# Cosine-similarity attention on one core: the first head pair head by head with its K only cast, the norms of the third and fourth pair by Newton steps, and new instruction orders on every engine

## The chip, the cores and the metric

The kernel runs on one core of a Trainium2 chip. The metric is the time of one execution in device microseconds (us). The kernel before takes 190.31 us, the median of three runs (190.27 to 190.34).

## The reference

Q, K and V are float32 arrays of 8 batches x 12 heads x 512 positions x 64 dimensions, tau is 0.1.

```python
Q_norm = Q / (np.linalg.norm(Q, axis=-1, keepdims=True) + 1e-10)
K_norm = K / (np.linalg.norm(K, axis=-1, keepdims=True) + 1e-10)
scores = np.einsum('bhqd,bhkd->bhqk', Q_norm, K_norm) / tau
weights = np.exp(scores - np.max(scores, axis=-1, keepdims=True))
weights = weights / (np.sum(weights, axis=-1, keepdims=True) + 1e-10)
return np.einsum('bhqk,bhkd->bhqd', weights, V).astype(np.float32)
```

Scores lie between -10 and 10, so the kernel takes exponentials without subtracting the maximum.

## The kernel before

**Work.** The 96 heads are worked in 48 pairs s = 0 to 47 (the text says pair 0 to pair 47, so "third pair" is pair 2). One pair has two heads h and four blocks c of 128 keys; a block's scores are 128 keys x 512 queries for each head. Q (w = 0) and K (w = 1) go through the same steps. For each pair:

- `LD` loads Q and K, 256 KB each (SP queue, L311; pair 0 in halves by head, L308, its K from ScalarE's queue), `LV` loads V (L314). Seventeen pairs of Q and K and ten of V fit in SBUF, so that `LD` of pair s waits for the last readers of pair s-17, and `LV` for the cast of pair s-10.
- `SQ` squares Q and K: one GpSimd instruction for the pair (L337); for pairs 0 to 3 split over ScalarE and GpSimd (L239, L241, L329, L331). `SSQ` adds up the squares of K (of Q too in pairs 1 to 3) in part with matmuls on TensorE (L354), `RED` finishes on VectorE (L361 behind `SSQ`, L365 from the squares, L245 in pair 0).
- `NEW` turns the sums into inverse norms for a group of pairs. Groups 0 to 3 are one pair each, later ones two, and the last one four. Most groups do it with an integer estimate and two Newton steps on VectorE (L389 to L398: `NEW` 0 to 8). The groups in `NORM_ON_ACT` do it on ScalarE: a logarithm `LOG` (L379, in pair 0 L248) and a small exponential of -0.5 times it (`NEW` 7, L382; in pair 0 `NRMS`, L252).
- `SCL` multiplies by the inverse norm and writes bfloat16 (L420; pair 0 L258). Q is done on VectorE, K on GpSimd, except the pairs in `K_ON_DVE`, whose K is done on VectorE too. tau is left to the exponential's scale.
- `TR` transposes on TensorE (L426; pair 0 L266 and L268), `EVA` copies the result to SBUF on VectorE (L434; pair 0 L279).
- `SCO` makes the scores of a block (two matmuls of 512 columns, L508) in one of two pairs of PSUM banks, so a block's score waits for the exponential two blocks earlier. `EXP` takes both heads' exponential in one ScalarE instruction (L531, 128x1024, with immediate scale 1/tau).
- `VC` casts V on GpSimd (L536). `PV` multiplies the exponentials with V and a column of ones, in four parts i of four matmuls for each head (L548). `RCP` and `NRM` divide by the sums on VectorE (L559, L561; last pair L587, L589), `ST` stores 256 KB (L565; last pair L593, in three pieces).

**Pair 0 before.** `head0` (L231) builds it. Both Q and K are scaled by inverse norms (K on GpSimd); the blocks 0 and 1 are done as four half exponentials (one head each, 128x512), the blocks 2 and 3 as full ones.

**The polynomial.** One block, c = 3 of pair 43, takes its exponential without ScalarE: two single matmuls `SCX` (L468), two conversions `X` for each head on VectorE (L473, L475), and six steps `Y` 0 to 5, the first four on GpSimd, the last two on VectorE (L486, L480). `PV` of pair 43 waits for `Y` 5.

**Order.** No scheduler runs at build time. `ORDER` holds one list of numbers per engine (SP, GpSimd, VectorE, TensorE, ScalarE), which is that engine's program in order; a number is the position of an operation in the sequence of `P.add` calls. The texts count the entries of such a list from 0. A negative number in TensorE's list is a filler matmul that only keeps the engine busy. `run()` (L42) derives the semaphore waits from each operation's needs. An engine works strictly in order, so an instruction that waits holds up all behind it in its list. On TensorE and ScalarE, waits for operations of the same engine are dropped unless the operation sets `.own`.

```python
o.waits = [self.ops[n] for n in o.needs]
if e in ("pe", "act") and not o.own:
    o.waits = [p for p in o.waits if p.eng != e]
```

Of the kernel before, what the change touches and what calls it, by code (L numbers as in the profile page):

```python
# [19 lines left out]
class Program:  # L20
# [22 lines left out]
    def run(self):  # L43
# [65 lines left out]
def bass_cosine_similarity_attention_kernel(  # L109
# [44 lines left out]
    t_k0 = sc_ps[:, 3, :].bitcast(bf16)[:, 0:SEQ].rearrange("p (t x) -> p t x", t=NT)  # L154
# [39 lines left out]
    P.fill = lambda e, n: e.matmul(out=sc_ps[:, 0, 0:n], lhsT=ident[:, :], rhs=warm_in[:, 0:n], start=True, stop=True)  # L194
# [26 lines left out]
    before = [[], []]  # L221
# [9 lines left out]
    def head0(TF):  # L231
        for h in range(2):
            at = -100 + h
            x4 = [xs[0][:, 8 * w + 4 * h : 8 * w + 4 * h + 4] for w in range(2)]
            for w in range(2):
# [4 lines left out]
                else:  # L240
# [5 lines left out]
            cols = lambda t, h=h: t[:, 0:16].rearrange("p (w x) -> p w x", w=2)[:, :, 4 * h : 4 * h + 4]  # L246
            P.add(("LOG", 0, h), "act", "ln", at + 0.4, [("RED", 0, 0, h), ("RED", 0, 1, h), "eps", "table"],
                  lambda e, cols=cols: e.activation(out=cols(ys[0]), in_=cols(xs[0]), func=ACT.Ln, bias=eps[:, :]))  # L248
            r_ps = sc_ps[:, 1, 0:4] if h == 0 else n_ps[:, 0, 128:132]
            for w in range(2):  # L250
                P.add(("NRMS", 0, w, h), "act", "sm_act", at + 0.5 + 0.01 * w, [("LOG", 0, h)],
                      lambda e, w=w, h=h, r_ps=r_ps: e.activation(  # L252
                          out=xs[0][:, 8 + 4 * h : 12 + 4 * h] if w else r_ps,
                          in_=ys[0][:, 8 * w + 4 * h : 8 * w + 4 * h + 4], func=ACT.Exp, scale=-0.5)).own = True
            for w in range(2):
                r = x4[1] if w else r_ps
                P.add(("SCL", 0, w, h), "pool" if w else "dve", "sclph" if w else "sclh", at + 0.6 + 0.1 * w, [("NRMS", 0, w, h)],
                      lambda e, w=w, h=h, r=r: e.tensor_tensor(  # L258
                          out=qn[0][:, w, :, h, :], in0=qk[0][:, w, h, :].rearrange("p (t d) -> p t d", t=NT),
                          in1=r.unsqueeze(2).to_broadcast([128, NT, DIM]), op=ALU.mult))  # L260
                out = t_k0 if w else t_ps[:, 0]

                def tr(e, w=w, h=h, out=out):
                    for t in range(NT):
# [7 lines left out]
                      [("SCL", 0, w, i) for i in range(h + 1)] + [("EVA", 0, w, 0) if h else None, "eye"], tr)  # L272
# [20 lines left out]
    def last_direct(s):  # L293
        d = [g for g in NORM_ON_ACT if g > 0 and direct_r(g)]
        return [("NEW", max(d), 7)] if d and group[s] not in NORM_ON_ACT and s < 12 else []

    def pair(s):
# [6 lines left out]
        for w, x in ((0, Q), (1, K)):  # L304
# [5 lines left out]
            P.add(("LD", s, w), "sp", "ld1" if s == 1 else "ld", s, [*([("SCL", 0, w, 0), ("SCL", 0, w, 1), ("SQ", 0, w, 0), ("SQ", 0, w, 1)] if s == R_QK else [key("SCL", s - R_QK, w), *(squares(s - R_QK, w) if s >= R_QK else [])])],  # L310
# [65 lines left out]
        if s == first[g] and g in NORM_ON_ACT:  # L376
# [6 lines left out]
                      out=n_ps[:, g % R_X, 128 : 128 + 2 * m] if direct else xs[g][:, 0 : 2 * m],  # L383
                      in_=ys[g % R_X][:, 0 : 2 * m], func=ACT.Exp, scale=-0.5)).own = True
            if not direct:
                P.add(("NEW", g, 6), "dve", "new", TF - 2.6, [("NEW", g, 7), ("NRMS", 0, 0, 1)],
                      lambda e: e.tensor_copy(out=n_ps[:, g % R_X, 128 : 128 + 2 * m], in_=xs[g][:, 0 : 2 * m]))
        elif s == first[g]:
# [15 lines left out]
            for k, step in enumerate(steps):  # L404
                needs = [("NEW", g, min(k, 6) - 1 if k < 8 else 7)] if k else reds + (free[1] if K_ON_DVE else [])
                if 6 <= k < 8:
                    needs += free[k - 6]
                P.add(("NEW", g, k), "dve", "new", TF - 4.9 - slack(s, M_NEW) + (M_STEP * (k - 7) if s > 8 else 0.23 * k), needs, step)
# [30 lines left out]
    def scos(s):  # L439
# [4 lines left out]
        return [("SCO", s, c) for c in range(NT)] if s else [("SCO", 0, c, h) for c in range(2) for h in range(2)] + [("SCO", 0, 2), ("SCO", 0, 3)]  # L444
# [4 lines left out]
    def exps(s, c):  # L449
# [4 lines left out]
        if s == 0 and c < 2:  # L454
# [39 lines left out]
    def rest(s):  # L494
# [3 lines left out]
        for c in range(NT):  # L498
            if (s, c) in OFF:
                poly(s, c, T0 - 3.0)  # L500
                continue
            turn = chunks.index((s, c))
            b = turn % 2

            for hs in ((0,), (1,)) if s == 0 and c < 2 else ((0, 1),):
                def sco(e, c=c, b=b, hs=hs):
                    for h in hs:
                        last = e.matmul(  # L508
                            out=sc_ps[:, 2 * b + h, :], lhsT=qt[iqt][64 * h : 64 * h + 64, 1, c, :],
                            rhs=qt[iqt][64 * h : 64 * h + 64, 0, :, :], start=True, stop=True)  # L510
                    return last

                needs = [("EVA", s)] if s else [("EVA", 0, w, h) for w in range(2) for h in (hs if c < 2 else (0, 1))]
                needs += exps(*chunks[turn - 2]) if turn >= 2 else []
                needs += [("SCL", 0, 0, 0)] if s == 0 and c == 0 and hs == (1,) else []
                P.add(("SCO", s, c) if len(hs) == 2 else ("SCO", s, c) + hs, "pe", "sco" if len(hs) == 2 else "sco1",
                      T0 + 0.9 * c + (0.5 * hs[0] if len(hs) < 2 else 0), needs, sco)
# [7 lines left out]
            for hs in ((0,), (1,)) if s == 0 and c < 2 else ((0, 1),):  # L525
                one = len(hs) == 1
                P.add(("EXP", s, c) + hs if one else ("EXP", s, c), "act", "exp1" if one else "exp",
                      T0 + 0.9 * c + (0.45 if s else 1.4) * hs[0] * one,
                      [("SCO", s, c) + hs if one and s == 0 else ("SCO", s, c)]
                      + [key("PV", s - R_ET, h, NT - 1) for h in range(2)] + ["table"],  # L530
                      lambda e, c=c, b=b, hs=hs: e.activation(  # L531
                          out=et[iet][:, c, hs[0] : hs[-1] + 1, :], in_=sc_ps[:, 2 * b + hs[0] : 2 * b + hs[-1] + 1, :],
                          func=ACT.Exp, scale=math.log(2.0) / UNIT if s in off_of else inv_tau))
# [9 lines left out]
        for h in range(2):  # L543
            for i in range(NT):
# [9 lines left out]
                need, due = sum((exps(s, c) for c in range(NT)), []), T0 + PERIOD + 0.9 * PV_AT[4 * h + i] + late(s)  # L554
# [64 lines left out]
K_ON_DVE = (1, 2, 3, 4, 9, 15, 21, 27, 33, 39)  # L619
# [20 lines left out]
def slack(s, most):  # L640
# [128 lines left out]
```

## Time and profile before

| what | value |
|---|---|
| median of the runs | 190.31 us |
| span of the profiled execution | 188.2 us |
| ScalarE (ACT) busy | 181.4 us, 96% |
| TensorE (PE) busy | 174.7 us, 93% |
| VectorE (DVE) busy | 169.6 us, 90% |
| GpSimd (POOL) busy | 160.8 us, 85% |
| moved by DMA | 50.75 MB, mean 270 GB/s |
| first half exponential starts | 8.16 us |
| first exponential of pair 1 / pair 2 starts | 12.81 / 16.78 us |
| last exponential ends | 184.86 us |
| last division ends | 186.02 us |

The span is that of one profiled execution, from its first instruction to its last; the 2.1 us between it and the median lie outside of the profile. Busy shares are means over the span. A group's line in the profile gives line, engine, operation, output and input tiles with shapes, the number of instructions, their busy time, the mean duration of one in ns, and the idle time of the engine just before them with what ended most of it. Times of single operations in the texts are read from the trace's timeline; an instruction's duration is longer than the distance to the next one where the two overlap (a full exponential lasts about 1.17 us, and one follows another every 0.917 us).

### The profile page before, as it was taken

Reading aid. Unit: us, or ns where it says so; the run is one execution under the profiler, and the core shown is the slowest. Engines: PE = TensorE matmul, PEld = TensorE weight load, DVE = VectorE, ACT = ScalarE, POOL = GpSimd, SP = SyncE. Lnnn points to the kernel's source line nnn. Section 1 sums busy time; section 2 is a strip of 40 time slices with the busy share of each in tenths; the row PEclk is TensorE's granted clock in tenths of the full one; section 3 lists DMA queues with packets and bytes.
Section 4 is the critical chain, followed back from the end, with each engine's and each line's share of the span. In section 5 each row is a group of like instructions: output and inputs, shape, how many; then the busy total and the mean of one; then the engine's idle time right before and its main releaser. Section 6 shows DMA issues by size and latency. Waiting matters only on the chain.

```text
span 188.2 us, 6658 instructions
## 1 busy us (share of the span) xinstructions
PE 174.7 (93%) x2710; PEld 109.9 (58%) x2710; DVE 169.6 (90%) x537; ACT 181.4 (96%) x213; POOL 160.8 (85%) x149
## 2 busy tenths in 40 slices
PE   6998999999999999999999899999999999797992
PEld 2655665666565666666666566666556566463662
DVE  2789999999999999999999989999899999989653
ACT  4899999999999999999999999999999999999992
POOL 4699989999999999999999999999999993695000
PEclk9999999999999999999999999999999999999999
DMA  5999999999999978999999997989779621111233
GB/s 151 346 353 352 348 358 327 269 331 365 379 382 368 309 236 271 317 360 322 368 380 381 376 317 237 326 292 296 254 215 354 204 73 55 60 56 59 101 125 112
DMA packets 52445, 50.75 MB, mean 270 GB/s; under 512 B 3136, under 2 KB 52416, under 8 KB 52416
## 3 DMA queue, kind: packets, MB, share of 16 engines
q1 hardware_dynamic: 51984, 50.02, 80.7%
q8 instruction: 21, 0.34, 0.7%
q10 hardware_dynamic: 432, 0.33, 0.5%
q14 instruction: 8, 0.07, 0.1%
HBM read 37.75 MB, written 12.58 MB: 267 GB/s over the span
## 4 chain that ended last, share of the span: by engine, by line
ACT 93%; DMA 3%; SPq 1%; issue 1%; PE 1%; DVE 1%
ACT et L531 92%; DMA qk<-in_Q_dram 3%; PE ops L576 1%; SPq L311 0%; SPq L308 0%; ACT ys L379 0%; DVE ob L589 0%; ACT sq L329 0%; ACT nps L382 0%; DVE rd L587 0%; PE tps L576 0%
## 5 line engine op out<-in xcount | busy, mean ns | idle before, releaser
L531 ACT ACTIVATE et<-scps 128x1024 bf16<-128x1024 f32 (+1 forms) x192 | 175.0, 1171 | 0.0
L337 POOL TENSOR_TENSOR sq<-qk 128x1024 bf16<-128x1024 f32 x44 | 82.9, 1900 | 0.7 <-DMA qk<-in_K_dram 0.5
L508 PE MATMUL scps<-qt 64*128 64x512 bf16 x382 | 75.2, 386 | 6.3 <-ACT et L531 3.0
L548 PE MATMUL ops<-vb,et 128*128 128x65 bf16 x1504 | 75.2, 194 | 2.1 <-ACT et L531 1.3
L548 PEld LDWEIGHTS ops<-vb,et 128*128 128x128 bf16 x1504 | 56.5, 98 | 30.8 <-issue 21.0
L420 POOL TENSOR_TENSOR qn<-qk,rk 128x512 bf16<-128x512 f32 x37 | 38.3, 1048 | 6.2 <-DVE rk L394 5.3
L561 DVE TENSOR_TENSOR ob<-ops,rd 128x256 f32<-128x256 f32 x94 | 39.0, 418 | 0.8
L420 DVE TENSOR_TENSOR qn<-qk,nps 128x512 bf16<-128x512 f32 x57 | 38.0, 676 | 0.4 <-ACT nps L382 0.4
L434 DVE COPY qt<-tps 128x1024 bf16<-128x1024 bf16 x47 | 32.2, 685 | 2.2 <-PE tps L426 1.6
L426 PE MATMUL tps<-ident,qn 128*128 128x128 bf16 x376 | 33.4, 220 | 0.1
L508 PEld LDWEIGHTS scps<-qt 64*128 64x128 bf16 x382 | 19.1, 92 | 24.1 <-ACT et L531 9.4
L365 DVE TENSOR_REDUCE nps<-sq 128x8 f32<-128x512 bf16 x46 | 31.0, 681 | 0.0
L536 POOL TENSOR_SCALAR vb<-vf 128x512 bf16<-128x512 f32 x48 | 29.6, 634 | 0.1
L426 PEld LDWEIGHTS tps<-ident,qn 128*128 128x128 bf16 x376 | 21.5, 98 | 10.3 <-issue 3.6
L559 DVE RECIPROCAL rd<-ops 128x4 f32<-128x4 f32 x94 | 16.5, 176 | 6.5 <-PE ops L548 4.2
L354 PE MATMUL ops<-sq,ident 128*128 128x64 bf16 x384 | 19.2, 193 | 0.0
L354 PEld LDWEIGHTS ops<-sq,ident 128*128 128x128 bf16 x384 | 14.4, 98 | 4.3 <-issue 2.7
L361 DVE TENSOR_REDUCE nps<-ops 128x8 f32<-128x64 f32 x42 | 9.0, 214 | 0.5 <-PE ops L354 0.4
L389 DVE TENSOR_TENSOR nps<-nps,ys 128x32 f32<-128x32 f32 (+1 forms) x30 | 6.3, 209 | 0.2
L390 DVE SCALAR_TENSOR_TENSOR nps<-nps,ys 128x32 f32<-128x32 f32 (+1 forms) x30 | 6.2, 208 | 0.2
L191 PE MATMUL ops<-warm_in,ident 128*128 128x512 bf16 x8 | 3.6, 631 | 1.4 <-POOL ident L181 1.4
L331 POOL TENSOR_TENSOR sq<-qk 128x512 bf16<-128x512 f32 (+1 forms) x4 | 3.7, 933 | 0.9 <-DMA qk<-in_K_dram 0.9
(61 smaller groups left out, 54.2 us busy)
## 6 DMA issues: line engine op xcount, KB each, us to landing
vf<-in_V_dram SPq DMA_DIRECT2D x48, 256.0 KB, 5.8
qk<-in_Q_dram SPq DMA_DIRECT2D x47, 256.0 KB, 4.9
qk<-in_K_dram SPq DMA_DIRECT2D x47, 256.0 KB, 6.0
out_dram<-ob SPq DMA_DIRECT2D x47, 256.0 KB, 4.0
qk<-in_Q_dram SPq DMA_DIRECT2D x2, 128.0 KB, 2.7
qk<-in_K_dram ACTq DMA_DIRECT2D x2, 128.0 KB, 3.0
out_dram<-ob SPq DMA_DIRECT2D x1, 128.0 KB, 1.7
out_dram<-ob ACTq DMA_DIRECT2D x1, 64.0 KB, 1.6
```

What stands on the lines that cost most here:

```text
L337: lambda e: e.tensor_tensor(out=sqf, in0=data, in1=data, op=ALU.mult))
L354: last = e.matmul(out=o_ps[bank][:, 320:384], lhsT=ident[:, :], rhs=sq[iqs][:, 8 * w : 8 * w + 8, 8 * k : 8 * k + 8], start=(k == 0), stop ...
L365: lambda e, w=w, dst=dst: e.tensor_reduce(out=dst, in_=sq[iqs][:, 8 * w : 8 * w + 8, :], axis=AX.X, op=ALU.add))
L420: lambda e, w=w, r=r: e.tensor_tensor(out=qn[iqn][:, w].rearrange("p t h d -> p h t d"), in0=qk[iq][:, w].rearrange("p h (t d) -> p h t d" ...
L426: last = e.transpose(t_ps[:, w, t, :], qn[iqn][:, w, t].rearrange("p h d -> p (h d)"), ident[:, :])
L434: lambda e: e.tensor_copy(out=qt[iqt][:, :, :, :].rearrange("p w t x -> p (w t x)"), in_=t_ps[:, :, :, :].rearrange("p w t x -> p (w t x)")))
L508: last = e.matmul(out=sc_ps[:, 2 * b + h, :], lhsT=qt[iqt][64 * h : 64 * h + 64, 1, c, :], rhs=qt[iqt][64 * h : 64 * h + 64, 0, :, :], sta ...
L531: lambda e, c=c, b=b, hs=hs: e.activation(out=et[iet][:, c, hs[0] : hs[-1] + 1, :], in_=sc_ps[:, 2 * b + hs[0] : 2 * b + hs[-1] + 1, :], f ...
L536: lambda e: e.tensor_scalar(out=vb[:, iq, :, :, 0:DIM].rearrange("p c h d -> p h c d"), in0=vf[iv][:, :, :].rearrange("p h (c d) -> p h c ...
L548: last = e.matmul(out=o_ps[h][:, 65 * t : 65 * t + 65], lhsT=et[iet][:, c, h, 128 * t : 128 * t + 128], rhs=vb[:, iq, c, h, :], start=(c = ...
L559: lambda e, h=h, grid=grid: e.reciprocal(out=rd[io][:, h, :], in_=grid[:, :, DIM]))
L561: lambda e, h=h, grid=grid: e.tensor_tensor(out=ob[io][:, h], in0=grid[:, :, 0:DIM], in1=rd[io][:, h, :].unsqueeze(2).to_broadcast([128, N ...
```

## The change

- **Pair 0 head by head.** All four blocks of head 0, then those of head 1, as eight half exponentials (128x512), in four PSUM banks, one for each block. The inverse norm of K is no longer multiplied into K: it is given to the exponential as a scale, a column of SBUF with one value for each partition (each key). So K is only cast to bfloat16 (`CST`, head 0 on ScalarE, head 1 on GpSimd) and transposed, into a bank of the output (`o_ps[0]`) in place of a score bank; pair 0's two `SCL` on GpSimd go. `LOG` is split by Q and K (four instructions of 128x4 for two of 128x8); its scale of 1/inv_tau on the sums gives Q's and K's inverse norms a factor of sqrt(1/tau) each, so that tau lies in the norms.
- **Norms.** Groups 2 and 3 leave `NORM_ON_ACT` and take Newton steps on VectorE. Group 1's small exponential becomes two, one for Q (`NEW` 6, to PSUM, for VectorE) and one for K (`NEW` 7, to SBUF, for GpSimd).
- **Moves.** K of pairs 1 and 3 is scaled on GpSimd instead of VectorE (`K_ON_DVE`). Of pair 1's squares of K, the half on ScalarE goes to VectorE; pair 2's squares of Q go from ScalarE to GpSimd.
- **Waits.** On TensorE and ScalarE a need for an operation of the same engine is kept if that operation is a DMA (a `slot`).
- **Orders.** All five lists are new: one filler matmul is left where six were; stores and casts of V stand out of the pairs' order (the cast of pair 26 is GpSimd's entry 64, before it was 86; of pair 40 entry 106, before 124); the last block's three pieces go 0, 1, 2, before 1, 0, 2.

The diff without the lists, cut to its core:

```diff
                 if e in ("pe", "act") and not o.own:
-                    o.waits = [p for p in o.waits if p.eng != e]
+                    o.waits = [p for p in o.waits if p.eng != e or p.slot is not None]
...
-    t_k0 = sc_ps[:, 3, :].bitcast(bf16)[:, 0:SEQ].rearrange("p (t x) -> p t x", t=NT)
+    t_k0 = o_ps[0][:, :].bitcast(bf16)[:, 0:SEQ].rearrange("p (t x) -> p t x", t=NT)
...
-    P.fill = lambda e, n: e.matmul(out=sc_ps[:, 0, 0:n], lhsT=ident[:, :], rhs=warm_in[:, 0:n], start=True, stop=True)
+    P.fill = lambda e, n: e.matmul(out=o_ps[1][:, 0:n], lhsT=ident[:, :], rhs=warm_in[:, 0:n], start=True, stop=True)
...
+            if CAST0[h] == "act":
+                emit = lambda e, a=cast_in, b=cast_out: e.activation(out=b, in_=a, func=ACT.Copy)
+            else:
+                emit = lambda e, a=cast_in, b=cast_out: e.tensor_copy(out=b, in_=a)
+            P.add(("CST", 0, h), CAST0[h], "cst" + CAST0[h], at, [("LD", 0, 1, h)], emit)
...
-            P.add(("LOG", 0, h), "act", "ln", at + 0.4, [("RED", 0, 0, h), ("RED", 0, 1, h), "eps", "table"],
-                  lambda e, cols=cols: e.activation(out=cols(ys[0]), in_=cols(xs[0]), func=ACT.Ln, bias=eps[:, :]))
+                P.add(("LOG", 0, w, h), "act", "ln", at + 0.4, [("RED", 0, w, h), "eps", "table"],
+                      lambda e, w=w, x4=x4, y4=y4: e.activation(out=y4[w], in_=x4[w], func=ACT.Ln, bias=eps[:, :], scale=1.0 / inv_tau))
...
-                P.add(("SCL", 0, w, h), "pool" if w else "dve", "sclph" if w else "sclh", at + 0.6 + 0.1 * w, [("NRMS", 0, w, h)],
+            P.add(("SCL", 0, 0, h), "dve", "sclh", at + 0.6, [("NRMS", 0, 0, h)],
...
+            if s == 0:
+                for h in range(2):
+                    rows = slice(64 * h, 64 * h + 64)
+                    P.add(("SCO", 0, c, h), "pe", "sco1", 0.5 * (c + NT * h),
+                          [("EVA", 0, w, h) for w in range(2)] + ([("EXP", 0, c, 0)] if h else []) + ([("SCL", 0, 0, 0)] if c == 1 else []),
+                          lambda e, c=c, rows=rows: e.matmul(
+                              out=sc_ps[:, c, :], lhsT=qt[iqt][rows, 1, c, :], rhs=qt[iqt][rows, 0, :, :], start=True, stop=True))
+                    P.add(("EXP", 0, c, h), "act", "exp1", 0.5 * (c + NT * h), [("SCO", 0, c, h), ("NRMS", 0, 1, h), "table"],
+                          lambda e, c=c, h=h: e.activation(
+                              out=et[iet][:, c, h, :], in_=sc_ps[:, c, :], func=ACT.Exp, scale=xs[0][:, 8 + 4 * h + c : 9 + 4 * h + c])).own = True
+                continue
...
-SQ_ON = {1: ("act", ("act", "pool")), 2: ("act", "pool"), 3: ("pool", "pool")}
+SQ_ON = {1: ("act", ("dve", "pool")), 2: ("pool", "pool"), 3: ("pool", "pool")}
+CAST0 = ("act", "pool")
-NORM_ON_ACT = {0: -90, 1: -45, 2: 0.5, 3: 6.0}
+NORM_ON_ACT = {0: -90, 1: -45}
-K_ON_DVE = (1, 2, 3, 4, 9, 15, 21, 27, 33, 39)
+K_ON_DVE = (2, 4, 9, 15, 21, 27, 33, 39)
```

Around pair 43, TensorE's list before, and after, in names of operations (pair, then block, or head and part):

```
before: SCO(44,3) PV(42,0,3) TR(46,1) SCO(45,0) PV(43,1,0) SCO(45,1) PV(43,1,1) PV(43,0,0) PV(43,1,2) ...
after:  SCO(44,3) PV(43,0,0) PV(43,0,1) PV(43,0,2) PV(43,1,0) PV(43,0,3) SCO(45,0) PV(43,1,1) PV(43,1,2) PV(43,1,3) SCO(45,1) ...
```

On VectorE, NRM(42,1) stood ahead of `Y` 4 and stands behind `Y` 5 after. On GpSimd, the entries 62 to 68 after are SCL(18,1), SQ(23), VC(26), VC(20), SCL(19,1), VC(19), SQ(24).

More of the change, by code (lines that the diff above doesn't have):

```diff
@@ L502, in rest, with sco @@
             turn = chunks.index((s, c))
             b = turn % 2
[L505 to L517, printed above, removed]
+            def sco(e, c=c, b=b):
+                for h in range(2):
+                    last = e.matmul(
+                        out=sc_ps[:, 2 * b + h, :], lhsT=qt[iqt][64 * h : 64 * h + 64, 1, c, :],
+                        rhs=qt[iqt][64 * h : 64 * h + 64, 0, :, :], start=True, stop=True)
+                return last
```

64 lines of the change are left out of this document (32 added, 32 removed), and 161 rows, old and new, of the table ORDER.

## The prediction

> **What bounds the kernel now.** I read the page's busy table and chain first, then the chain in order of time, then ScalarE's timeline at the start, then VectorE's and TensorE's around the one block whose exponential is a polynomial. The page:
>
> ```profile
> ACT 93%; DMA 3%; SPq 1%; issue 1%; PE 1%; DVE 1%
> ...
> L531 ACT ACTIVATE et<-scps 128x1024 bf16<-128x1024 f32 (+1 forms) x192 | 175.0, 1171 | 0.0
> L337 POOL TENSOR_TENSOR sq<-qk 128x1024 bf16<-128x1024 f32 x44 | 82.9, 1900 | 0.7 <-DMA qk<-in_K_dram 0.5
> ...
> L420 POOL TENSOR_TENSOR qn<-qk,rk 128x512 bf16<-128x512 f32 x37 | 38.3, 1048 | 6.2 <-DVE rk L394 5.3
> ...
> L536 POOL TENSOR_SCALAR vb<-vf 128x512 bf16<-128x512 f32 x48 | 29.6, 634 | 0.1
> ```
>
> The set bound is ScalarE's exponentials (L531): 93% of the chain, no idle time ahead of them. GpSimd is nearly as full. The chain in order of time (start, us, what):
>
> ```profile
> 11.13 0.65 issue
> ...
> 15.04 168.78 ACT et L531 x184
> 183.83 0.05 issue
> ```
>
> From 15.04 on 184 full exponentials run end to end, 168.78/184 = 0.917 each. That stream can't be shortened by this change, which leaves their number; it can only start earlier, or be interrupted. ScalarE's timeline up to it (start, us, line, tile):
>
> ```profile
> 8.16 0.60 ACT L531 ACTIVATE et<-scps 128x512 bf16<-128x512 f32 x1
> 8.77 0.31 ACT L379 ACTIVATE ys<-xs,eps 128x16 f32<-128x16 f32 x1
> 9.11 0.19 ACT L382 ACTIVATE nps<-ys 128x16 f32<-128x16 f32 x1
> 9.23 1.56 ACT L531 ACTIVATE et<-scps 128x512 bf16<-128x512 f32 x3
> 10.68 0.31 ACT L379 ACTIVATE ys<-xs,eps 128x16 f32<-128x16 f32 x1
> ...
> 11.78 0.20 ACT L382 ACTIVATE nps<-ys 128x16 f32<-128x16 f32 x1
> 11.89 1.94 ACT L531 ACTIVATE et<-scps 128x1024 bf16<-128x1024 f32 x2
> 13.75 0.31 ACT L379 ACTIVATE ys<-xs,eps 128x16 f32<-128x16 f32 x1
> 13.96 1.00 ACT L531 ACTIVATE et<-scps 128x1024 bf16<-128x1024 f32 x1
> 14.87 0.18 ACT L382 ACTIVATE nps<-ys 128x16 f32<-128x16 f32 x1
> ```
>
> The reader is to see the start at 8.16 and three logarithms with their small exponentials (groups 1, 2, 3) between the blocks. Pair 2's first exponential starts at 16.78; I measure the head by that point. The span is 188.2; the median of the runs is 190.31, so 2.1 lie outside the span, which I leave as they are.
>
> **Head: first exponential.** Before, it waits for K's GpSimd scaling (5.34), transposes, copy and score (7.74 to 8.13). After, K is only cast and Q's chain is left: square 3.39 to 3.81, reduction 0.42 (to 4.28), logarithm 0.31 (to 4.62), exponential 0.19 (to 4.84), scaling 0.41 (to 5.28), four transposes at the slow clock 0.63 (to 5.96), copy 0.42 (to 6.42), score, 512 columns at the slow clock (the warm-up's 128x512 took 0.63), to 7.10, each with the hand-off of some 0.05 that the rows show. First exponential 7.14, **1.02 earlier**.
>
> **Head: pair 1.** ScalarE's own work from 7.14: eight halves at 0.49 (ends of L531's first ones), one logarithm 0.20, three small exponentials 0.11 each (issue intervals): 4.45, so 11.6. A half now reads its scale from a column of SBUF, which no exponential here does. Lower bound nothing (the operand is fetched while the one before runs); upper: the logarithm with its bias column took 0.30 to 0.31, the small exponential 0.21, so 0.09 each, 8 x 0.09 = 0.7, up to 12.3. I take 0.4, midway: 12.0. But EXP(1,0) needs pair 1's K, which the change gives to GpSimd: squares SQ(2,0), SQ(2,1) 7.69 to 9.69 (1.00 each), SCL(1,1) to 10.73 (1.04), transposes 0.39 (11.18), copy 0.69 (12.00), score 0.39 (12.44). So EXP(1,0) starts at 12.45, not 12.81: **0.36 earlier**, whatever the columns cost within their bounds.
>
> The Trainium skill, "ScalarE: Activation LUTs", section "What ACT_TABLE_LOAD costs", says that each [128,1] pointer operand adds about 93 ns to an ACTIVATE, and so speaks against the half exponentials; the logarithm's row agrees with it. By the one reading the head's ScalarE work ends at 11.6, by the other at 12.3; by it the first block of pair 1 can't start before 12.35, and the full gain in rival C is closed, which is why I give that part of C little.
>
> **Head: groups 2 and 3.** Two logarithms and two small exponentials leave ScalarE: 2 x (0.20 + 0.10) = 0.6 of its time, of which one pair fell before 12.81 (in a wait, the 0.65 "issue"), the other between 12.81 and 16.78: four blocks took 3.97 for 4 x 0.917 = 3.67, 0.30 removed. They return as 17 Newton steps of about 0.19 on VectorE (a dependent one every 0.22), 3.7 in all, between 11 and 16, where the timeline shows it idle for some 0.7 and the two scalings moved to GpSimd free 2 x 0.59. In VectorE's new order pair 2's scaling and copy just make EXP(2,0) and SCL(3,1) at 16.99 to 18.04 on GpSimd just makes EXP(3,0): hidden with less than 0.1 to spare; without that cover 0.2 to 0.4. Gain at pair 2: 0.36 + 0.30 - 0.05 = **0.6**; both ends 0.2 and 1.0.
>
> **Pair 43, the polynomial.** VectorE, then TensorE, before:
>
> ```profile
> 170.59 0.42 DVE L561 TENSOR_TENSOR ob<-ops,rd 128x256 f32<-128x256 f32 x1
> 170.93 2.10 DVE L486 SCALAR_TENSOR_TENSOR et<-xz,xw 128x1024 bf16<-128x1024 f32 x1
> 173.06 0.69 DVE L480 TENSOR_TENSOR et<-et,xp 128x1024 bf16<-128x1024 bf16 x1
> ```
> ```profile
> 172.87 0.39 PE L508 MATMUL scps<-qt 64*128 64x512 bf16 x2
> 173.81 0.30 PE L548 MATMUL ops<-vb,et 128*128 128x65 bf16 x4 [0.55 <-DVE et L480]
> 174.04 0.39 PE L508 MATMUL scps<-qt 64*128 64x512 bf16 x2
> ```
>
> The score at 172.87 is pair 45's first; only behind it comes PV(43), which waits for the polynomial's end (173.75). In the new order PV(43,0,0 to 3) and PV(43,1,0) stand **before** that score, and PV(43,1,0) waits for NRM(42,1), which has moved behind the polynomial on VectorE. From E, the end of EXP(41,1): score SCO(41,3) and SCX(43,1) behind it, E+0.77; its two conversions on VectorE (0.68 and 0.69) E+2.2; the polynomial takes 9.15 in the trace (164.60 to 173.75), E+11.35; NRM(42,1) 0.35, PV(43,1,0) and PV(43,0,3) 0.12 each with hand-offs, so the score starts at E+12.0, ends at 12.4, and EXP(45,0), with 1.02 from start to end out of an empty queue, ends at E+13.44. Due are 14 blocks, 14 x 0.917 = E+12.83. **Loss 0.6**. Bounds: 0 (were the polynomial 0.6 quicker) and 0.8 (were the conversions to wait for VectorE).
>
> **GpSimd's casts of V.** The new order takes V casts far ahead of need. VC(26) ran at 99.06, its data landed at 86.02. Now it is GpSimd's entry 64: from SQ(4) at 13.3, 20 squares at 1.85, 17 casts at 0.585 and 13 scalings at 1.0 (intervals of the rows above) make 59.9, so it comes at 73.2 to 73.5. Its load is SP's entry 95 (102 before). SP waits for store ST(9) (entry 71) until pair 9 is done, about 53.1, and 24 transfers follow. Landings under load are 0.69 to 0.75 apart. With the few transfers then in flight, ST(9) lands at about 56, LV(26) at 73 to 74.9. Behind VC(26) stand VC(20), SCL(19,1), VC(19) and SQ(24); TensorE has TR(19,1) ahead of SCO(18,3). There is about 1 us of cover: a start up to 74.5 costs nothing, one at 75 costs 0.6 to 0.9. VC(40) repeats it: GpSimd reaches it at 119.3, its load lands between 117.6 and 120.9, cost 0 to 1.2. Together 0 to 2; I take **0.6**, as the middle of the landings is near where it begins to cost.
>
> **Tail and the rest.** Last pieces in another order: -0.03. Stores out of order: ST(42), 256 KB, is issued shortly before the last pair's; 0 to 0.2, I take 0.1, since its transfer (0.7) is ahead of theirs. Waits on ScalarE's own K loads (`slot`) end before the squares anyway: 0, hidden by the chain at 3.4.
>
> Sum: -0.6 + 0.6 + 0.6 + 0.0 = +0.6: span 188.8, time **190.9**.
>
> **Rivals.**
> - A, not slower: both V loads land in time, so nothing waits. Place GpSimd's entries 64 and 106, price 0.6 in all, deciding point VC(26) starting by 74.5. For it: GpSimd's 44 squares wait 0.5 in all for a DMA now, its 48 casts 0.1, and 0.71 per transfer gives 73. Against: after SP's pause near 33 us, 23 transfers in a row took 18.2 (landed 36.03 to 54.25), which gives 74.9. Time 190.3.
> - C, faster: the polynomial's lateness doesn't show, or the head gains its full 1.0. The first needs it to end by E+10.75; its six steps in their measured lengths alone make 8.7 of the 9.15, which is against it. Time 190.31 - 0.6 = 189.7.
> - D, the head doesn't do what it says: only one filler matmul is left, and TensorE's columns stay slow (0.107 for 128, not 0.056, which came at 7.0) for, I assume, as long again as the warm-up's 3.6, until 10.6. Seven half scores, transposes and sums of squares are about 2 us longer on its queue, half of it in waits: +1.1, partly in place of the head's gain; 191.3. Against: the transposes fill 4.9 to 7.0 as densely as the fillers did. The Trainium skill, "TensorE: Matmul & The Clock Gate", Part 1, ties the release to a free-running window of about 3.4 us of activity: one window more would end at 10.4, with the same price. The rows fit it so far: slow from 1.44, fast by 7.0.
> - Both waits in full, with the loss at 43: 192.3.
>
> **How the numbers follow.** Forecast 0.43, A 0.30, C 0.17, D 0.06, both waits in full 0.04. 0.2% (0.38 us) is about what a measurement of this kernel can tell from no change: faster below 189.93, slower above 190.69. C is faster, and 0.03 of A (head at its better end); same is the rest of A and 0.05 of the forecast's low end; the rest is slower. Range 189.6 to 191.9: it takes in C's centre, A, and V waits up to 1.6. Where the forecast holds, 190.5 to 191.6.
>
> **What would show it.** First exponential at 7.1; EXP(1,0) at 12.45, released by a score behind pair 1's copy; pair 2's at 16.2; a gap of 0.6 ahead of pair 45's first block, ended by a score behind PV(43); waits of GpSimd's cast for DMA at 73 to 75 and 119 to 121. Wrong if GpSimd never waits, if the stream of 184 has no hole, or if TensorE's rows stay at 0.107 past 7.5.

## The result

The changed kernel takes **195.51 us** (median of 6 runs, 195.10 to 196.83) against 190.36 for the kernel before beside it; ratio 1.028, 95% interval 1.025 to 1.031. It is slower by 5.2 us. The forecast was 190.9 and its range ended at 191.9: wrong by far. Here and below the ratios compare only undisturbed runs of both kernels, so a ratio need not be the quotient of the medians beside it.

The profiled execution took 196.4 us, its span is 194.5 (188.2 before), so it is one of the longer runs. The first lines of its page that answer to those of before:

```profile
ACT 42%; DVE 22%; POOL 21%; PE 10%; issue 4%; DVEq 0%; POOLq 0%
...
L541 ACT ACTIVATE et<-scps 128x1024 bf16<-128x1024 f32 x186 | 172.1, 1085 | 5.4 <-PE scps L525 5.2
...
L546 POOL TENSOR_SCALAR vb<-vf 128x512 bf16<-128x512 f32 x48 | 29.4, 626 | 5.7 <-DMA vf<-in_V_dram 5.6
```

The chain was 93% ScalarE and now runs through three more engines. The exponentials, which never waited, now wait 5.4 us, 5.2 of it for scores. GpSimd's casts of V wait 5.6 us for their DMA (0.1 in all before). To place the loss I lined up the end of each exponential in the two traces. The columns are how much later the changed kernel is than before, in us:

| at the end of | late by | new loss since the row above |
|---|---|---|
| pair 2's first block | -0.26 | head: -0.26 |
| pair 6's last block | -0.20 | 0.06 |
| pair 8's first block | 0.15 | 0.35 |
| pair 18's third block | 0.15 | 0 |
| pair 18's last block | 3.02 | 2.87 |
| pair 20's first block | 4.39 | 1.37 |
| pair 30's third block | 4.46 | 0.07 |
| pair 32's first block | 6.04 | 1.58 |
| pair 44's last block | 6.28 | 0.24 |
| last block | 6.35 | 0.07 |

Three places make the loss: pairs 18 to 20 (4.2), 30 to 32 (1.6) and 6 to 8 (0.35). GpSimd's timeline ahead of the first, and ahead of the second (start, us, line; in brackets its idle time before):

```profile
72.51 1.89 POOL L341 TENSOR_TENSOR sq<-qk 128x1024 bf16<-128x1024 f32 x1
78.05 1.21 POOL L546 TENSOR_SCALAR vb<-vf 128x512 bf16<-128x512 f32 x2 [3.65 <-DMA vf<-in_V_dram]
...
124.86 1.21 POOL L546 TENSOR_SCALAR vb<-vf 128x512 bf16<-128x512 f32 x2 [1.59 <-DMA vf<-in_V_dram]
```

The row at 78.05 is the cast of pair 26, GpSimd's entry 64. GpSimd reaches it at 74.40 and stands until its V has landed at 77.97. Pair 19's K scaling is behind it. TensorE and ScalarE a little later:

```profile
76.99 0.42 PE L558 MATMUL ops<-vb,et 128*128 128x65 bf16 x8
80.32 0.40 PE L433 MATMUL tps<-ident,qn 128*128 128x128 bf16 x4 [2.92 <-POOL qn L427]
```
```profile
73.65 4.79 ACT L541 ACTIVATE et<-scps 128x1024 bf16<-128x1024 f32 x5
81.21 1.94 ACT L541 ACTIVATE et<-scps 128x1024 bf16<-128x1024 f32 x2 [2.77 <-PE scps L525]
84.18 6.75 ACT L541 ACTIVATE et<-scps 128x1024 bf16<-128x1024 f32 x7 [1.04 <-PE scps L525]
```

The stages behind it (start:end, then the width, the busy time of PE, PEld, DVE, ACT and POOL, and last the granted clock of TensorE, the share of the DMA engines and GB/s):

```profile
80.00:81.00 1.00, 0.68 (x10) 0.50 (x10) 0.24 (x1) 0.00 (x0) 1.00 (x3) 1.00 1.04 336
81.00:82.00 1.00, 1.00 (x12) 0.39 (x10) 1.00 (x3) 0.79 (x1) 1.00 (x1) 0.79 1.09 379
82.00:83.00 1.00, 0.86 (x15) 0.69 (x14) 0.74 (x2) 1.00 (x2) 1.00 (x2) 0.50 1.09 365
```

TensorE stands 2.92 us at pair 19's transposes, which are in order ahead of pair 18's last score, and ScalarE 2.77 behind it. The second hole, 1.04, falls into the time in which TensorE's granted clock, 1.00 until then, is at 0.50 (81.6 to 85.0 us). I take it for a consequence of that; e3_st9 comes back to it. The casts of pairs 40 (1.59 us of waiting, 123.27 to 124.86) and 10 (0.37, 30.94 to 31.31) make the other two steps in the same way. V of pair 26 is first used at 113.66; nothing needed that cast at 74.

### The profile page after: what moved, and what is told of

The parts are those of the page before. It is cut to its first block, busy times and chain, and to the rows that moved or that the text cites. A ratio compares the mean times of both kernels' runs of the same rounds, so it can differ in the third digit from the quotient of the medians.

```text
span 194.5 us, 6650 instructions
## 1 busy us (share of the span) xinstructions
PE 174.0 (89%) x2705; PEld 109.2 (56%) x2705; DVE 171.0 (88%) x553; ACT 182.8 (94%) x213; POOL 163.2 (84%) x151
## 4 chain that ended last, share of the span: by engine, by line
ACT 42%; DVE 22%; POOL 21%; PE 10%; issue 4%; DVEq 0%; POOLq 0%
ACT et L541 40%; POOL sq L341 11%; POOL qn L427 6%; DVE qn L427 4%; POOL vb L546 3%; DVE qt L441 3%; DVE nps L369 3%; DVE ob L571 3%; PE ops L558 3%; PE scps L525 3%; PE ops L191 2%; ACT et L517 2%; PE tps L433 1%; DVE nps L395 1%; DVE nps L394 1%
## 5 line engine op out<-in xcount | busy, mean ns | idle before, releaser
L541 ACT ACTIVATE et<-scps 128x1024 bf16<-128x1024 f32 x186 | 172.1, 1085 | 5.4 <-PE scps L525 5.2
L525 PE MATMUL scps<-qt 64*128 64x512 bf16 x374 | 73.7, 389 | 8.1 <-ACT et L541 5.2
L427 POOL TENSOR_TENSOR qn<-qk,rk 128x512 bf16<-128x512 f32 x38 | 39.5, 1043 | 3.8 <-DVE rk L399 3.7
L433 PE MATMUL tps<-ident,qn 128*128 128x128 bf16 x376 | 34.1, 221 | 5.9 <-POOL qn L427 5.0
L427 DVE TENSOR_TENSOR qn<-qk,nps 128x512 bf16<-128x512 f32 x55 | 36.5, 677 | 0.7 <-ACT nps L391 0.7
L525 PEld LDWEIGHTS scps<-qt 64*128 64x128 bf16 x374 | 18.2, 93 | 25.6 <-ACT et L541 10.1
L365 DVE TENSOR_REDUCE nps<-ops 128x8 f32<-128x64 f32 x46 | 9.9, 216 | 0.5 <-PE ops L358 0.4
L394 DVE TENSOR_TENSOR nps<-nps,ys 128x32 f32<-128x32 f32 (+2 forms) x34 | 7.1, 208 | 0.7
L395 DVE SCALAR_TENSOR_TENSOR nps<-nps,ys 128x32 f32<-128x32 f32 (+2 forms) x34 | 7.0, 207 | 0.4
L335 POOL TENSOR_TENSOR sq<-qk 128x512 bf16<-128x512 f32 (+1 forms) x5 | 5.1, 1045 | 1.5 <-DMA qk<-in_K_dram 1.5
```

Source lines behind the costliest of these rows:

```text
L427: lambda e, w=w, r=r: e.tensor_tensor(out=qn[iqn][:, w].rearrange("p t h d -> p h t d"), in0=qk[iq][:, w].rearrange("p h (t d) -> p h t d" ...
L433: last = e.transpose(t_ps[:, w, t, :], qn[iqn][:, w, t].rearrange("p h d -> p (h d)"), ident[:, :])
L525: last = e.matmul(out=sc_ps[:, 2 * b + h, :], lhsT=qt[iqt][64 * h : 64 * h + 64, 1, c, :], rhs=qt[iqt][64 * h : 64 * h + 64, 0, :, :], sta ...
L541: lambda e, c=c, b=b: e.activation(out=et[iet][:, c, :, :], in_=sc_ps[:, 2 * b : 2 * b + 2, :], func=ACT.Exp, scale=math.log(2.0) / UNIT i ...
```

## The experiments

The kernels were built from the changed kernel or the one before by moving entries of `ORDER`; the diffs name operations, not numbers. A kernel is timed against before on the same chip; medians of before there were 190.3 to 190.9, so ratios are compared, not times.

**Theory and rival.** T: early casts of V wait for loads, and the loads are late because SP stood at a store. R: the loss comes from TensorE's or VectorE's new order, or the transfers run at their limit and no order of SP would help.

### e1_vc26: one cast moved

```diff
 # GpSimd
-SQ(23) VC(26) VC(20) SCL(19,1) ... VC(24) VC(30) SCL(24,1)
+SQ(23) VC(20) SCL(19,1) ... VC(24) VC(30) VC(26) SCL(24,1)
```

> The changed kernel with one entry of GpSimd's list moved: the cast of V of pair 26 goes from entry 64 to behind the cast of pair 30 (entry 82). Theory (the lost time is GpSimd standing at this cast until its V has landed at 77.97): the 3.65 us wait ahead of it and the late blocks of pairs 18 to 20 go, about 4.2 us, unless the wait at pair 40's cast grows because GpSimd gets there earlier and its load does not: 191.3 without that, up to 195 with it. Rival (the engines were late there for another reason, VectorE's or TensorE's new order): below 1 us changes, 194.5 to 195.5.

Median 193.51, ratio 1.016 (1.012 to 1.020). The steps at pairs 18 to 20 are 0.00 in its trace; pair 40's cast still waits 1.4 and costs 1.4 at pairs 30 and 31. The theory holds, and the rival falls as far as TensorE's and VectorE's orders go. The median is 2.2 above the theory's 191.3. Of that the trace shows 1.3 in the head, which ends 1.03 late beside before where that of the changed kernel ended 0.26 early: pair 1's first block is 0.40 late (its Q landed at 6.87, for 5.74 in the changed kernel), and a new step of 0.7 stands at EXP(1,3), to which e6_fill comes back.

### e2_vc_all: all three casts moved

```diff
 # GpSimd, beside e1_vc26
-SQ(8) VC(10) SCL(7,1)         VC(36) SCL(31,1) VC(40) VC(39)
+SQ(8) SCL(7,1)                VC(36) SCL(31,1) VC(39)
+VC(9) VC(10) SCL(11,1)        VC(43) VC(40) VC(38)
```

> The changed kernel with three entries of GpSimd's list moved: the casts of V of pairs 10, 26 and 40 go behind those of pairs 9, 30 and 43. Theory (these three casts wait for their loads, 0.37, 3.65 and 1.59 us, and nothing else of weight is lost): what is left is the head's gain of 0.25 and some 0.3 of small losses, 190.2 to 190.5. Rival (the loads are late for the squares too, so another instruction of GpSimd waits in the casts' place): 191.5 to 194.

Median 191.63 (190.39 to 192.74), ratio 1.006 (1.004 to 1.009): from 2.8% to 0.6%. The steps at 6 to 8, 18 to 20 and 30 to 32 are all gone. It misses the expected 190.2 to 190.5 by some 1.2: its profile has a step of 0.8 at EXP(1,3), and small ones, 0.5 at pair 23 and 0.4 at pair 36, whose cause was not sought.

### e3_st9: SP does not stand at the store

```diff
 # SP
-ST(6) ST(9) LD(22,1) LV(20) ... ST(8) ST(7) LV(22)
+ST(6) LD(22,1) LV(20) ... ST(8) ST(7) ST(9) LV(22)
```

> The changed kernel with one entry of SP's list moved: the store of pair 9 goes from entry 71 to behind the store of pair 7, ten entries later, so that SP does not stand for 4.3 us (49.51 to 53.84) while loads could be issued. GpSimd's casts stay where they are. Theory (the load of V 26 is late because the transfers dried up behind that store and came back slowly, 24 in 21.3 us): it lands 2 to 3.5 us sooner, and 2 to 3.5 of the 4.2 us at pairs 18 to 20 come back, 192 to 193.5. Rival (the transfers run at their limit through the whole stretch and the pause cost nothing): lands as before, 195 to 195.5.

The changed kernel's SP queue, where one line of 4.72 us holds two stores. The first issue, ST(6), takes 1.61 of it, to 51.12; then SP waits 2.72 us for pair 9, and ST(9) goes out at 53.84:

```profile
48.80 0.66 SPq L315 DMA_DIRECT2D qk<-in_Q_dram  x1
49.51 4.72 SPq L575 DMA_DIRECT2D out_dram<-ob  x2
54.28 0.46 SPq L315 DMA_DIRECT2D qk<-in_K_dram  x1
```

By stages (columns as above), first the changed kernel, then e3_st9:

```profile
54.00:56.00 2.00, 2.00 (x37) 1.27 (x36) 1.97 (x11) 2.00 (x3) 2.00 (x2) 1.00 0.83 265
56.00:58.00 2.00, 1.81 (x35) 1.14 (x35) 2.00 (x8) 2.00 (x3) 2.00 (x4) 1.00 0.99 335
58.00:60.00 2.00, 2.00 (x38) 1.44 (x38) 2.00 (x5) 2.00 (x4) 2.00 (x2) 1.00 0.74 249
60.00:63.00 3.00, 3.00 (x61) 2.06 (x57) 2.97 (x14) 3.00 (x5) 3.00 (x3) 1.00 0.88 250
```
```profile
58.00:60.00 2.00, 1.82 (x31) 1.16 (x28) 2.00 (x6) 2.00 (x4) 2.00 (x2) 1.00 1.09 369
60.00:63.00 3.00, 3.00 (x55) 2.02 (x51) 3.00 (x12) 3.00 (x4) 3.00 (x4) 1.00 1.09 380
```

GpSimd at the cast of pair 26 in e3_st9, without idle time before it:

```profile
75.14 1.23 POOL L546 TENSOR_SCALAR vb<-vf 128x512 bf16<-128x512 f32 x2
```

Behind the pause the DMA moves 249 to 335 GB/s for nine microseconds, where 369 to 384 is had without it. V of pair 26 lands at 74.07 instead of 77.97, before GpSimd gets there (75.14), and the step at pairs 18 to 20 is 0.00. So T's second half holds too: at this place neither the early cast nor the pause costs anything alone. How much the pause costs is less sure than these two traces make it look: in the five other traces with the changed kernel's SP order (e1, e2, e5, e6, e7) V of pair 26 lands at 76.0 to 78.4, so its price is 2 to 4.3 us.

The median is only 194.35, ratio 1.018 (1.014 to 1.022), outside the expected 192 to 193.5. The trace is that of its longest run, 195.48. In it the cast of pair 10 waits 1.17 and pairs 6 to 8 cost 1.15 (0.37 and 0.35 in the changed kernel's trace), the cast of pair 40 waits 1.78, the clock falls to a half for 6.8 us behind it, and pairs 30 to 32 cost 4.0. In the traces of the changed kernel and of e1_vc26 a wait of 1.59 and 1.41 at that cast brought no fall of the clock and cost 1.6 and 1.4: a wait alone costs its own length, and what comes on top goes with the clock. The other runs have no trace; three with a mean clock of 0.991 took 194.0 to 194.6, the one with 0.999 took 192.37.

### e4_head_only: the new head, the old order behind it

```diff
 # each engine but SP: the changed kernel's order up to about 17 us, then before's
-SCL(3,1) VC(2) VC(1) SQ(6) VC(5) ...      # GpSimd, changed kernel
+SCL(3,1) VC(2) VC(1) VC(3) SQ(6) VC(4) ... # GpSimd, e4
```

> The head of the change (pairs 0 to 3 in the new way and the new order up to about 17 us) with the order of the kernel before for all that follows, on every engine; SP's order is that of before from its start. The trace of the changed kernel has pair 2's first exponential 0.26 ahead of before. Theory (the head is a small gain, the loss lies in the rest of the orders): 190.0 to 190.2. Rival (the old order does not fit the new head: the V casts that it holds back, or two more scalings of K on GpSimd, make it late in the first 40 us): 190.4 to 192.

Median 191.14, ratio 1.006 (1.003 to 1.008). This is what the rival had. Its profile loses nothing between pairs 5 and 44, but 0.94 at EXP(3,1) and 1.0 at pair 45. So the orders make the large loss, and the head is no gain either.

### e9_head_fixed: repairing that

```diff
 # GpSimd, from e4_head_only
-VC(0) SQ(4) SQ(5) SCL(3,1) VC(2) VC(1)
+VC(0) VC(1) SQ(4) SQ(5) SCL(3,1) VC(2)
 # TensorE: + 4 fillers of 256 columns ahead of SSQ(1,1), 5 ahead of SCO(1,0)
```

> As e4_head_only (the head of the change, the order of before for the rest), with two repairs: GpSimd's cast of V of pair 1 goes from behind pair 2's to behind pair 0's, and nine matmuls of 256 columns keep TensorE busy in the head as in e6_fill. Theory (of e4_head_only's profiled loss of 2.4 us against the span of before 0.94 was PV(1) waiting for that cast ahead of pair 3's second score, 1.0 the clock that fell behind the polynomial, the rest a late load of pair 1's Q): the step at pair 3 is gone, 189.9 to 190.6. Rival (the old order has no room for the new head in more places): further steps between pairs 3 and 8, 190.8 or more.

Median 191.53, ratio 1.006 (1.003 to 1.009). The step at EXP(3,1) is still 0.94, so my cause for it was wrong. A new one of 0.55 stands at pair 2's first block, made by the repair: the moved cast puts off the squares of pair 4 on GpSimd, and TensorE has SSQ(4,1), which waits for them, ahead of that score. The trace gives another cause for the 0.94, which no run tests: PV(1) stands ahead of that score and waits for NRM(0,1) (21.88 to 22.30), which the old order of VectorE has behind pair 3's copy; that copy waits for the K scaling moved to GpSimd and the Newton steps, and runs at 20.16 instead of 16.91. The new head delivers pair 3 three microseconds later, and the old order has no room for that.

### e5_scale: what a column as scale costs

```diff
-                              ... func=ACT.Exp, scale=xs[0][:, 8 + 4 * h + c : 9 + 4 * h + c])).own = True
+                              ... func=ACT.Exp, scale=1.0)).own = True
```

This kernel leaves out K's inverse norms in pair 0; only its time is read.

> The changed kernel with the three casts of V moved as in e2_vc_all, and pair 0's eight half exponentials with a constant scale of 1.0 in place of the column of K's inverse norms; so pair 0's K is not normalised, its time only is read. Theory (each half pays 0.085 us for the column: its spacing is 0.575, that of before's halves 0.49, and they run one behind the other up to pair 1): spacing 0.49, EXP(0,2,1) ends 0.5 to 0.7 sooner against the first half's start, pair 1's first block 0.2 to 0.5 sooner, then held by pair 1's own scores. Rival of the record (GpSimd's squares and K scaling hold pair 1 at 12.45 whatever a half costs): spacing smaller, pair 1's first block where it is within 0.1.

ScalarE with the constant, then with the column (e6_fill, the same there but for TensorE's fillers):

```profile
9.28 2.52 ACT L517 ACTIVATE et<-scps 128x512 bf16<-128x512 f32 x5
12.33 1.94 ACT L541 ACTIVATE et<-scps 128x1024 bf16<-128x1024 f32 x2 [0.52 <-PE scps L525]
```
```profile
9.84 2.98 ACT L517 ACTIVATE et<-scps,xs 128x512 bf16<-128x512 f32 x5
12.84 1.94 ACT L541 ACTIVATE et<-scps 128x1024 bf16<-128x1024 f32 x2
```

Halves are 0.49 apart against 0.575, 0.085 for each column; a single one takes 0.60 against 0.69. The Trainium skill, "ScalarE: Activation LUTs", section "What ACT_TABLE_LOAD costs", gives 93 ns for a pointer operand; the trace agrees. But with the constant ScalarE waits 0.52 for pair 1's score: from the first half to pair 1 it takes 5.44 us against 5.51. The chain over GpSimd of my forecast, which ends in that score, is the second bound, hardly behind the first. Median 191.33, ratio 1.006 (1.003 to 1.009), no faster than e2_vc_all. My theory got the price, the rival the consequence.

### e6_fill: the clock in the head

```diff
 # TensorE, from e2_vc_all: + 4 fillers of 256 columns ahead of SSQ(1,1)
+    P.add(("KEEP", 1), "pe", "fill", 0, [("RED", 2, 1)], keep)   # 5 of them, ahead of SCO(1,0)
```

> The changed kernel with the three casts of V moved as in e2_vc_all, and nine matmuls of 256 columns more on TensorE in its two idle stretches of the head (four ahead of pair 1's sums of squares, five between pair 1's transposes and its first score). Theory (in e2_vc_all's trace the granted clock is 0.50 from 13 to 16.3 us because the new head leaves TensorE idle from 9 to 13; the runs spread by 2.3 us since it does not fall in each of them): the clock stays at 1.00, EXP(1,3) comes 0.8 to 1.0 sooner than in e2_vc_all, the median falls to 190.5 to 191.0 and the spread below 1.5. Rival (the fall is due to a phase that the fillers do not touch): clock at 0.5 as before in some runs, 191.3 to 192.

Stages of e2_vc_all, then of e6_fill (columns as above):

```profile
8.00:10.00 2.00, 1.53 (x28) 0.97 (x28) 1.10 (x4) 1.89 (x8) 2.00 (x3) 1.00 1.09 378
10.00:12.00 2.00, 1.58 (x24) 0.89 (x20) 1.82 (x8) 2.00 (x5) 2.00 (x3) 1.00 1.10 350
12.00:13.00 1.00, 0.41 (x4) 0.12 (x4) 0.93 (x5) 0.94 (x3) 1.00 (x2) 0.99 1.11 349
13.00:14.00 1.00, 1.00 (x12) 0.56 (x13) 0.74 (x3) 1.00 (x2) 0.92 (x3) 0.50 1.10 346
```
```profile
8.00:10.00 2.00, 2.00 (x35) 1.35 (x33) 0.94 (x4) 1.89 (x8) 1.99 (x3) 1.00 1.08 381
...
13.00:14.00 1.00, 0.92 (x20) 0.61 (x18) 0.94 (x3) 1.00 (x2) 0.96 (x2) 1.00 1.10 346
```

TensorE was busy 3.5 of the 5 us before 13 in e2_vc_all, and its clock is at a half until 16.4 us. With the fillers it stays at 1.00, and EXP(1,3), 0.99 late beside before in e2_vc_all, is 0.15 early. Median 190.81 (190.33 to 191.66, spread 1.3 for 2.4), ratio 1.0035 (1.0019 to 1.0051), as expected. That the fillers did it is likely, not shown: of the seven traces with this head and no fillers only two, e1_vc26 and e2_vc_all, have the fall at 13 us, and by runs it is 3 of 12 in e2_vc_all with a mean clock of 0.991 or less (192.5 to 192.6) against none of 12. The median of the other nine runs of e2_vc_all is 191.27, so the fall is a part of the difference only; its longest run, 192.74, has a clock of 1.000. What is left of the slowness in e6_fill are steps of 0.05 to 0.2 along the new order, 0.7 in sum in its trace.

### e7_y4: why the loss at pair 45 did not come

```diff
 # GpSimd, from e2_vc_all
-SCL(47,1) SCL(44,1) Y(43,0) Y(43,1) Y(43,2) Y(43,3)
+SCL(44,1) Y(43,0) Y(43,1) Y(43,2) Y(43,3) SCL(47,1)
```

> The changed kernel with the three casts of V moved as in e2_vc_all, and GpSimd's scaling SCL(47,1) put behind the polynomial's fourth step, where the kernel before has it, so that it runs beside VectorE's step Y4. Theory (Y4 took 2.10 us in before because GpSimd worked beside it, and 1.23 in the changed kernel where GpSimd had nothing left; that is why the forecast loss at pair 45 did not come): Y4 takes 2.0 to 2.2 again, EXP(45,0) comes 0.5 to 0.8 late, and the time rises by as much over e2_vc_all: 192.0 to 192.5. Rival (Y4's length has another cause, its order on VectorE or the clock): Y4 1.2 to 1.3, no change.

VectorE at the polynomial's end in the changed kernel, then VectorE and GpSimd in e7_y4, and last the same scaling in the kernel before, whose Y4 begins at 170.93:

```profile
176.72 1.23 DVE L493 SCALAR_TENSOR_TENSOR et<-xz,xw 128x1024 bf16<-128x1024 f32 x1 [0.34 <-POOL xw L486]
...
177.98 0.69 DVE L487 TENSOR_TENSOR et<-et,xp 128x1024 bf16<-128x1024 bf16 x1
```
```profile
171.65 1.22 DVE L493 SCALAR_TENSOR_TENSOR et<-xz,xw 128x1024 bf16<-128x1024 f32 x1 [0.33 <-POOL xw L486]
...
172.91 1.42 DVE L487 TENSOR_TENSOR et<-et,xp 128x1024 bf16<-128x1024 bf16 x1
```
```profile
171.69 2.08 POOL L427 TENSOR_TENSOR qn<-qk,rk 128x512 bf16<-128x512 f32 x1
```
```profile
170.91 1.04 POOL L420 TENSOR_TENSOR qn<-qk,rk 128x512 bf16<-128x512 f32 x1
```

Y4 is 1.22 again, not the 2.10 I expected; instead the scaling, begun 0.04 after it, takes 2.08 for 1.04, and Y5 1.42 for 0.69. In before the scaling began 0.02 ahead of Y4 and Y4 paid. So the two exclude each other: whichever begins first runs at its own pace and the other is prolonged by it. The Trainium skill, "SBUF — State Buffer", section "SBUF: two separate sides", says it so: a shared pair of ports, exclusively locked for an instruction, asked for by a VectorE operation with two SBUF inputs and by GpSimd; these rows agree with it. Y5 ends 0.7 late, EXP(45,0) comes 1.17 late, and with the clock falling behind it pair 45's blocks lose 2.2. Median 192.69, 0.2 above the expected range, ratio 1.013 (1.010 to 1.016) against 1.006 for e2_vc_all, 0.7% more; the profiled run took 193.43. So the loss that I forecast is real in this TensorE order when the polynomial is longer by 0.7; the length that I gave it was wrong.

### e10_head_fixed_y4 and e11_before_y4: the same entry in the old order

```diff
 # GpSimd, from e9_head_fixed and from before
-SCL(45,1) Y(43,0) ... Y(43,3) SCL(47,1)
+SCL(45,1) SCL(47,1) Y(43,0) ... Y(43,3)
```

> As e9_head_fixed, and GpSimd's scaling SCL(47,1) goes ahead of the polynomial's first step, so that GpSimd has nothing to do beside step Y4 on VectorE. Theory (Y4 and that scaling exclude each other, so Y4 takes 1.22 alone and 2.10 beside it): Y4 1.2 to 1.3, Y5 ends 0.8 to 0.9 sooner, TensorE's wait of 0.5 ahead of PV(43) is gone, so its clock does not fall there in any run: the median 0 to 0.4 below e9_head_fixed, the slowest runs 1 lower. Rival: Y4 as before, no difference.

> The kernel before with that one entry of GpSimd's list moved: SCL(47,1) ahead of the polynomial's first step. Theory: Y4 1.2 to 1.3 instead of 2.10, and since the stream of exponentials had no hole there, the time is the same within 0.2%, unless the clock fell there in some runs of before. Rival (the scaling ahead delays the polynomial by its 1.0 and eats the gain): Y5 ends where it did.

Y4 is 1.23 in both, and Y5 ends 11.97 behind EXP(41,1) in both, 11.93 in before: the scaling ahead of the polynomial eats its whole gain, as e11's rival had it. Medians 191.90, ratio 1.008 (1.006 to 1.011), and 190.50, ratio 1.002 (1.000 to 1.005); e10 is 0.4 above e9, where 0 to 0.4 below was expected. The clock falls to a half at pair 45 in both profiles (1.0 us each), so that expectation failed too. The changed kernel can have both: the last norms (group 18, pairs 44 to 47) give K's inverse norms 1.3 sooner against the exponentials, 1.53 ahead of the end of EXP(41,1) for 0.23 in before, so that all four scalings are done when the polynomial starts. (From pair 20 on every group of norms has four pairs, not the last one alone.)

### e8_before: before, a second time

> The kernel before, unchanged, for a second look on this chip. Theory (the runs on this chip have pair 1's Q landing at 6.4 to 6.9 us, 5.6 in the profile of before on another; the old head is less tied to that load): Q of pair 1 lands at 6.4 to 6.9, the first exponential is 0 to 0.5 later than 8.16, the granted clock stays at 1.00 from 8 us on, 190.3 to 191. Rival (the old head pays for the late load like the new one): first exponential 0.7 to 1.0 later, 191 to 191.5.

One run, 189.94. Pair 1's Q landed at 5.84, not late, so the question was not tested. In the traces of e11 and e12, whose head is that of before, Q landed at 6.08 and 6.12, and pair 1's first block ended 0.03 early and 0.11 late; no trace has a landing near 6.9 under the old head. In this run the exponentials are 0.36 to 0.42 earlier than in the first profile, which shows by how much the head of one and the same kernel moves.

### e12_before_keep: the clock at the polynomial

```diff
 # TensorE, from before: 5 matmuls of 256 columns ahead of PV(43,1,0)
+    P.add(("KEEP", 43), "pe", "fill", 0, [("NRM", 42, 1)], keep)
```

> The kernel before with five matmuls of 256 columns more on TensorE, in its wait of 0.5 us ahead of PV(43,1,0). Theory (the polynomial's end leaves TensorE idle; in some runs of before, those with a granted clock below 0.99, the clock falls there and costs about 0.8 us; the same fall took 1.0 in e4_head_only, e10 and e11): no run of this kernel has a clock below 0.99, none is above 191.0 for that reason, the median is unchanged within 0.2%. Rival (the fall comes from a longer stretch with few matmuls, which five of them do not fill): one run in six or so at 191 to 191.6 as in before.

Median 190.59 (189.87 to 191.32) against 190.89 for before; ratio 0.998 (0.995 to 1.000). None of its 12 runs has a mean clock below 0.99, 5 of the 17 of before beside them do, at 191.3 to 192.2. So the fillers do what was expected of the clock; one run still takes 191.32, at a clock of 1.000. Whether the median gains is not shown, since the interval reaches 1.

## Why the prediction was wrong, point by point

- **The casts of V** is the step that failed. "Together 0 to 2; I take 0.6": measured 6.2 (4.2 at pair 26, 1.6 at pair 40, 0.35 at pair 10, which I had not listed). Place, order and deciding point were right: GpSimd came at 74.40 (forecast 73.2 to 73.5), and what counted was whether the load landed by then. The term mis-sized is the landing: ST(9) landed at 56.7 (about 56 forecast), the 24 transfers behind it took 21.3 us, where I allowed 17 to 18.9, and V came at 77.97, not at 73 to 74.9. My upper end was the pace behind a pause in the trace of before, 0.79 each; here they were 0.89 apart. I had reckoned with no slower pace than that behind ST(9); the pause there cost 3.9 us by e3_st9, 2 to 4.3 by the other traces. And I priced a late start with the cover of TensorE's queue alone; the idle TensorE then lost its clock (0.50 for 3.4 us), about 1 us more. The rival "both waits in full" named the mechanism, at 192.3 and 0.04, so range and chance were both too small.
- **Pair 43** (0.6): measured 0.00 at pair 45's first block. Order and waits were as forecast (the score stood behind PV(43), at E+11.45 instead of E+12.0); the mis-sized term is "the polynomial takes 9.15 in the trace": it took 8.20, since Y4 had no GpSimd beside it: GpSimd's new order puts SCL(47,1), which ran beside Y4 before, ahead of the polynomial, and I had not looked at that. The conversions ended at E+2.48, not E+2.2, which took back 0.3. A duration copied from a row holds only with its neighbours; e7_y4 shows both.
- **First exponential 7.14**: 7.05, right, and so was the chain of rows behind it up to the copy. The score then began 0.2 later than I had it, but ran 0.38 instead of 0.63, since the clock was released at 6.50; that the two nearly cancel is luck.
- **Pair 1 at 12.45**: 12.71. The chain that I named for it ran as I named it and came 0.23 late: pair 1's score ended at 12.67 (forecast 12.44). ScalarE's own work ended at the same point, the last half at 12.69: 8 halves at 0.575 (I took 0.4 for the columns; 8 x 0.085 = 0.7 was right), and 0.27 of waiting for pair 1's sums in front of LOG(1) that I had left out. Without the columns pair 1 comes 0.07 sooner against the first half (e5_scale), so "whatever the columns cost" held within 0.1.
- **Gain at pair 2, 0.6**: 0.26, the 0.36 at pair 1 being 0.1 and the 0.30 behind it 0.16.
- **Newton steps and scalings moved**: hidden in this trace, as forecast; with the old order they are not (e9_head_fixed, 0.94).
- **Rival D**, the clock: not at 7 us, where TensorE was fast in time, but at 13 us in some runs, 0.8 to 1.0 (the traces of e1_vc26 and e2_vc_all). The fillers that the change takes out ran before 7.9 us, so it is not shown that they would have helped there.
- **Tail**: 0.07 in all, right.

What stays open is why the DMA came back slowly after the pause: SP's issues at 55.83, 61.48 and 65.89 took 1.65, 1.66 and 2.01 us instead of 0.5, and no run tells what held them. Issues of 1.4 to 1.6 us also stand where SP had not paused (at 27.27 and 34.14), so they may have nothing to do with it.

## What to carry to other kernels

An engine works in order, so an instruction that waits for a load holds up everything behind it, needed or not. On an engine that is 85% busy, put such an instruction where its data has long landed, and check the landing against the worst queue, with the pauses that the issuing queue takes for stores, not against its best rate. A duration read from a profile is that of an instruction among its neighbours; where an order changes, ask which of them ran beside it on a shared resource. And a stall in a kernel of matmuls costs more than itself when TensorE's clock falls behind it, which happens in some runs and not in others.

## What the runs showed of the hardware

- VectorE's 128x1024 SCALAR_TENSOR_TENSOR from two SBUF tiles takes 1.22 us alone and 2.10 behind a GpSimd scaling begun 0.02 earlier; begun 0.04 ahead of it, the scaling takes 2.08 for 1.04.
- TensorE's clock fell to half after stretches that were far from idle: 3.5 of 5 us busy ahead of 13 us in e2_vc_all, and about 0.5 us of waiting at the polynomial. It did not fall in each run of one kernel, and e4_head_only, with 3.4 of the same 5 us busy, kept 1.00 there in its trace. In the 14 traces the granted clock changes only at whole multiples of 3.41 us from its first release, which lies between 4.09 and 7.44 us, and it stays at half for one such window (two in e3_st9). The Trainium skill, "TensorE: Matmul & The Clock Gate", Part 1, has a free-running window of 3413 ns; the traces agree with it.
- By a count from the matmul records, the window ahead of each of the eight falls within a kernel held 2,460 to 4,452 matmul columns (a score of one head is 512). Of the 724 full-clock windows without a fall six held 4,452 or fewer, and the fullest 7,929. Four of the eight falls lie at the polynomial, with 4,376 to 4,452; the five fillers of e12_before_keep add 1,280 there. So what seems to count is how full such a window is, and where the windows lie against the kernel differs from run to run. No experiment set this limit.
- After SP's pause the DMA moved 249 to 335 GB/s for nine microseconds before it came back to 366, with loads still in SP's list; in five other traces with that pause it was 222 to 332, without the pause 369 to 384 (one trace, e3_st9).
